# RWKV stage: r and k products dealt out by a table of rounds, and TensorE's order pinned to the program's

## The chip, the cores and the metric

The kernel runs on one core of a Trainium2 chip. The metric is the device time of one execution in microseconds (us); the time of a kernel is the median of several executions. The core has five engines, each with a queue of its own that it works through from the front: TensorE (PE in the profile, with its weight loads as PEld), VectorE (DVE), ScalarE (ACT), GpSimd (POOL) and SyncE (SP), which issues most of the DMAs. Engines wait for each other on semaphores.

## The reference

A decoder trunk of two layers on 256 tokens of width 2048, in float32: one RWKV-7 time-mixing layer and one attention layer, each followed by a squared-ReLU MLP. The change lies in the time mixing, which is

```
xs = h + (token_shift(h) - h) * mu            # six mixtures
r, k, v = xs[0] @ W_r, xs[1] @ W_k, xs[2] @ W_v
decay = exp(-exp(w_log)); a = sigmoid(...); g = sigmoid(xg @ g1) @ g2
for each token t, per head of 64 channels (32 heads):
    sa = S @ (-kk_t)
    S  = S * w_t + sa (kk_t * a_t)^T + v_t k_t^T
    y_t = S @ r_t
out = ((groupnorm(y) + bonus) * g) @ w_o
```

The kernel does not go token by token. It takes the sequence in two chunks of 128 tokens and solves a triangular system in each: products of decayed r, k and kk make 128x128 matrices, a lower triangle is inverted (16x16 blocks first, then 32, 64 and 128 by doubling), and the state S passes from the first chunk to the second.

## The kernel before

The 2048 channels are 16 tiles of 128 (two heads each). A tile's work is the generator `rwkv_tile(i)`, in 27 steps that end at its `yield`s. Three tiles are in flight (`LONG`), each begun nine rounds of the main loop after the one before (`STAGGER`), so that the three stand nine steps apart; nine rounds of the loop are called a round below, and a round in that sense begins one new tile. The steps that matter here, with their products on TensorE by the names of the profile:

- steps 1 to 5: `wa` (decay and a), the scan `cum`, `st`, and the operands AR, bt, kt on VectorE
- step 6: `pm` from bt (L658), made into MB by ScalarE and POOL; step 7: `tr` of bt and kt; step 8: A32, Dg and the four Z on ScalarE and VectorE
- step 9: the two `ar` products from Z (L710), and `pm` from kt
- steps 10 to 12: the X chain, 15 turns of `xt` = ar * X (L722) and X += xt (L723) on VectorE, each of which needs the one before; `pg` (the gate) and the first `prhs` (L739) in between; at its end T16 on ScalarE and Tn on VectorE (L748)
- step 13: `pW` from Tn (L753); steps 14 to 19: `pN`, `pW`, `pT` in turn, the doubling, each through ScalarE or VectorE to the next, to the finished inverse Tt
- steps 20 to 24: `pu`, `psS`, `prhs`, `py`, the solve and the state, chunk by chunk
- steps 25 to 27: the group norm (`tr` of V, mean, var, `yt`) and the output

Since three tiles advance together, a turn of the main loop runs for instance steps 4, 13 and 22.

Beside the tiles go the r and k products of the next tile, `project_rk(i)`: `rk` in the profile. Each of the two has 16 k-tiles of 128 rows, a k-tile is three matmuls (high and low halves of the weights and of the inputs, L213 to L215), so 32 k-tiles and 96 products a tile. The weights are loaded as `raw`, 1024 columns at a time are rounded on ScalarE (`whi`, L162), and the rest is taken off on VectorE (`wlo`, L163), into two buffers (`WB`) that all weights of the stage share. At each such unit `pump` gives VectorE some of the modulation's matrix-vector products, the ada work (L310, `raw` with `crow`, 1024 columns each).

The loop gives `fill`, the generator of the products, a fixed number of turns after each turn of the tiles: 16 / 9, of two k-tiles each.

The program is traced in this order and then handed to a scheduler, which sets each engine's order by its own costs. Only inside `with tc.manual_schedule(engines={PE})` does TensorE's order follow the program's; before, the RWKV stage has no such block. After tile 15 is begun, `fill` is `out_start`, part of the output projection, at `PACE` turns a step.

Of the kernel before, what the change touches and what calls it, by code (L numbers as in the profile page):

```python
# [33 lines left out]
STAGGER = 9  # L34
XV = 2
RATE_R = 0.85
RATE_T = 0.75
PACE = 2.5
RATE_M = 0.68
RATE_L = 0.25  # L40
RATE_H = 1.0
# [35 lines left out]
def trunk_kernel(ctx: ExitStack, tc: tile.TileContext, a, out, dbg=None):  # L77
# [83 lines left out]
    def hilo(hi, lo, x):  # L161
        ACT.copy(hi, x)  # L162
        return DVE.tensor_sub(lo, x, hi.bitcast(F32))  # L163
# [3 lines left out]
    def load(src, n=2048, ahead=False):  # L167
        raw = room_for[0]() if room_for[0] else None
        if raw is not None:
            SP.dma_start(raw[:, :n], src)  # L170
            return raw
        more = split.get("more")
        if more and not ahead:
            split["turn"] += 1
        raw = (more if more and not ahead and split["turn"] > EARLY else wp).tile([P, 2048], F32, tag="raw", name="raw")
        SP.dma_start(raw[:, :n], src)
        return raw
# [5 lines left out]
    def pump(n):  # L183

        due[0] += n
        while due[0] >= 1:
            due[0] -= 1
            if next(ada_it[0], 0) == 0:
                return
# [22 lines left out]
    def mm3w(ps, wh, wl, xh, xl, start, stop):  # L212
        PE.matmul(ps, wh, xh, start=start, stop=False)  # L213
        PE.matmul(ps, wh, xl, start=False, stop=False)  # L214
        PE.matmul(ps, wl, xh, start=False, stop=stop)  # L215
# [162 lines left out]
    with ExitStack() as s0:  # L378
# [8 lines left out]
        def xs_at(w, z, kt):  # L387
            return XS[kt // 4][:, 2 * w + z, kt % 4, :]
# [152 lines left out]
        with ExitStack() as s2:  # L541
# [9 lines left out]
            def tmp(tag, shape=(T,), bufs=1, dt=F32):  # L551
                return p5.tile([P, *shape], dt, tag=tag, name=tag, bufs=bufs)
# [13 lines left out]
            def project_rk(i):  # L566

                ps = banks["rk"].tile([P, 512], F32, tag="rk", name="rk")
                res = []
                for w, name in enumerate(("wr", "wk")):  # L570
                    raw = load(a[name][i])
                    o = slice(w * T, (w + 1) * T)
                    for half in range(2):
                        hi = split["hi"].tile([P, 1024], F32R, tag="whi", name="whi")
                        lo = split["lo"].tile([P, 1024], F32R, tag="wlo", name="wlo")
                        hilo(hi, lo, raw[:, half * 1024 : half * 1024 + 1024])
                        pump(rate[0])
                        for j in range(8):
                            kt = half * 8 + j
                            s = slice(j * P, (j + 1) * P)  # L580
                            mm3w(ps[:, o], hi[:, s], lo[:, s], xs_at(w, 0, kt), xs_at(w, 1, kt), kt == 0, kt == KT - 1)
                            if j % 2:
                                yield
                    res.append(tmp("rk"[w] + "S"))
                    ACT.copy(res[w], ps[:, o])  # L585
                rks[i] = res
# [292 lines left out]
            def out_start():  # L879

                for i in range(KO):
                    split_o(i)
                    yield
                for n in range(4):
                    pss = [banks[k].tile([P, 512], F32, tag=k, name="pos") for k in ("rk", "mm")]
                    for g in range(KO // 4):
                        for half, (hi, lo) in enumerate(unit(a["wo"][n, g])):
                            for j in range(2):
                                kt = g * 4 + half * 2 + j
                                s = slice(j * 512, (j + 1) * 512)  # L890
                                for t in range(2):
                                    q = slice(t * P, (t + 1) * P)
                                    mm3(pss[t], o_h[:, kt, q], o_l[:, kt, q], hi[:, s], lo[:, s], kt == 0, kt == KO - 1)
                                    yield
                    for t in range(2):
                        ACT.copy(yo[:, t, n * 512 : (n + 1) * 512], pss[t])
# [4 lines left out]
            for _ in project_rk(0):  # L901
                pass
            flying, nxt, steps = [], 0, 0
            fill, owed, pace = iter(()), 0.0, 16 / STAGGER
            while nxt < KT or flying:
                if nxt < KT and len(flying) < LONG and steps >= STAGGER * nxt:
                    for _ in fill:
                        pass
                    flying.append(rwkv_tile(nxt))
                    nxt += 1  # L910
                    if nxt < KT:
                        fill = project_rk(nxt)
                    else:
                        o_h = p1.tile([P, KT, T], F32R, tag="xs0", name="oh")
                        o_l = p1.tile([P, KT, T], F32R, tag="xs1", name="ol")
                        yo = p1.tile([P, KT, T], F32R, tag="xs2", name="yo").bitcast(F32).rearrange(
                            "p (t k) c -> p t (k c)", t=2)
                        fill, pace = out_start(), PACE
                        rate[0] = RATE_T
                steps += 1  # L920
                for g_ in list(flying):
                    if next(g_, 0) == 0:
                        flying.remove(g_)

                owed += pace if flying else 48
                while owed >= 1:
                    owed -= 1
                    next(fill, 0)
            for _ in fill:
                pass  # L930
            for i in range(KO, KT):
# [299 lines left out]
    cs = cp.tile([P, 2, 2, 32], F32, name="cs")  # L1231
    rx = mlp(0, x, rx, RATE_M, rotary_tables)
    if dbg:
# [330 lines left out]
```

## Time and profile before

| what | us |
|---|---|
| median of three runs | 2627.69 (2624.5 to 2628.51) |
| the profiled execution | 2610.6 |
| its span | 2608.9 |
| TensorE busy | 2510.7 (96% of the span) |
| VectorE busy | 1950.6 (75%) |
| ScalarE busy | 1314.7 (50%) |
| r and k products (`rk`), first and last start | 212.0 and 683.1 |
| first and last `ar` product of the stage | 244.9 and 714.6 |

A profile line of the timeline reads: start, duration, engine, line, instruction, what is written and read, shape, how often, and in brackets how long the engine stood idle before it and for whom. Matmuls are pipelined and their ends are modelled, so that a run of 256-column products shows 0.28 us for each while one starts every 0.12; the distance of starts is what one costs. In a table of stretches each engine has its busy time and its count of instructions; after the engines come the granted share of TensorE's clock, the busy share of the DMA engines and GB/s.

### The profile page before, as it was taken

How to read it: one execution, taken by the hardware profiler on the slowest of the kernel's cores; microseconds unless marked ns; L12 is line 12 of the kernel's file. 1: busy time of each engine (PE TensorE's matmuls, PEld its weight loads, DVE VectorE, ACT ScalarE, POOL GpSimd, SP SyncE). 2: the span in 40 equal slices, each digit the busy share in tenths (PEclk: the TensorE clock that was granted, in tenths of full speed). 3: DMA queues.
4: the chain of work that ended last, by engine and by line, in shares of the span. 5: the costliest groups of instructions: out<-in, count | busy, mean ns of one | idle time of the engine just before them, and what ended most of it. 6: DMA issues, size and time to landing. Idle time of an engine off the chain costs nothing.

```text
span 2608.9 us, 39245 instructions
## 1 busy us (share of the span) xinstructions
PE 2510.7 (96%) x15048; PEld 2077.0 (80%) x15048; DVE 1950.6 (75%) x3823; ACT 1314.7 (50%) x2361; POOL 65.9 (3%) x150
## 2 busy tenths in 40 slices
PE   6998999999997999999999999999899999999998
PEld 3667888888776888888888878788788888888886
DVE  4797888888877788888888868777677655565555
ACT  4555666666745444444444446544544444444443
POOL 0000111011100000000000000000000000000000
PEclk9999999999999999999999999999999999999999
DMA  9755444444466588888888834657657555555553
GB/s 374 304 192 202 155 170 157 166 158 171 167 227 258 201 337 316 329 332 325 333 316 331 328 140 139 211 178 263 219 210 260 192 193 187 187 191 194 187 186 127
DMA packets 87885, 594.54 MB, mean 228 GB/s; under 512 B 10128, under 2 KB 14480, under 8 KB 16784
## 3 DMA queue, kind: packets, MB, share of 16 engines
q1 hardware_dynamic: 87696, 592.03, 62.9%
q8 instruction: 118, 1.93, 0.3%
q14 instruction: 71, 0.58, 0.1%
HBM read 589.89 MB, written 2.10 MB: 227 GB/s over the span
## 4 chain that ended last, share of the span: by engine, by line
PE 87%; DVE 7%; ACT 3%; DMA 2%; issue 1%; POOL 0%; SPq 0%; DVEq 0%; ACTq 0%
PE pup L223 17%; PE pd L208 9%; PE pd L210 9%; PE pd L209 9%; PE pup L224 9%; PE rk L213 2%; PE rk L215 2%; PE rk L214 2%; PE pm L658 2%; DVE wlo L163 2%; PE po L209 1%; PE po L210 1%; PE po L208 1%; PE pv L209 1%; PE pv L210 1%
## 5 line engine op out<-in xcount | busy, mean ns | idle before, releaser
L162 ACT CAST whi<-raw 128x1024 fp32r<-128x1024 f32 x729 | 743.7, 1023 | 882.7 <-PE pd L210 356.3
L163 DVE TENSOR_TENSOR wlo<-raw,whi 128x1024 fp32r<-128x1024 f32 x729 | 865.2, 1189 | 430.1 <-ACT whi L162 427.0
L223 PE MATMUL pup<-h,whi 128*128 128x512 f32 x1920 | 677.8, 398 | 0.0
L224 PE MATMUL pup<-h,wlo 128*128 128x256 f32 x1920 | 539.7, 281 | 0.0
L223 PEld LDWEIGHTS pup<-h,whi 128*128 128x128 f32 x1920 | 361.0, 188 | 88.2
L208 PE MATMUL pd<-whi,uh 128*128 128x512 f32 x1024 | 399.2, 390 | 0.0
L210 PE MATMUL pd<-whi,ul 128*128 128x512 f32 x1024 | 398.9, 390 | 0.0
L209 PE MATMUL pd<-wlo,uh 128*128 128x512 f32 x1024 | 398.8, 389 | 0.0
L310 DVE SCALAR_TENSOR_TENSOR raw<-raw,crow 128x1024 f32<-128x1024 f32 x320 | 388.5, 1221 | 10.5 <-DMA raw<-in_adat_dram 10.2
L224 PEld LDWEIGHTS pup<-h,wlo 128*128 128x128 f32 x1920 | 363.4, 189 | 0.5
L210 PEld LDWEIGHTS pd<-whi,ul 128*128 128x128 f32 x1024 | 192.3, 188 | 40.2
L208 PEld LDWEIGHTS pd<-whi,uh 128*128 128x128 f32 x1024 | 192.3, 188 | 39.9
L209 PEld LDWEIGHTS pd<-wlo,uh 128*128 128x128 f32 x1024 | 192.3, 188 | 39.5
L213 PE MATMUL rk<-xs,whi 128*128 128x256 f32 x512 | 155.2, 303 | 2.8 <-ACT rS L585 2.2
L215 PE MATMUL rk<-xs,wlo 128*128 128x256 f32 x512 | 149.6, 292 | 2.0 <-DVE wlo L163 2.0
L214 PE MATMUL rk<-xs,whi 128*128 128x256 f32 x512 | 147.1, 287 | 0.0
L213 PEld LDWEIGHTS rk<-xs,whi 128*128 128x128 f32 x512 | 98.5, 192 | 13.8 <-issue 8.9
L215 PEld LDWEIGHTS rk<-xs,wlo 128*128 128x128 f32 x512 | 98.4, 192 | 4.7 <-DVE wlo L163 2.8
L214 PEld LDWEIGHTS rk<-xs,whi 128*128 128x128 f32 x512 | 98.5, 192 | 0.9
L722 DVE TENSOR_TENSOR xt<-ar,X 128x60 f32<-128x60 f32 (+14 forms) x240 | 49.5, 206 | 17.5 <-ACT ar L711 14.8
L1180 DVE TENSOR_TENSOR ya<-pd,ya 128x512 f32<-128x512 f32 x96 | 61.5, 682 | 0.0
L209 PE MATMUL pv<-wlo,xsv 128*128 128x512 f32 x128 | 52.8, 413 | 5.5 <-DVE wlo L163 5.3
(431 smaller groups left out, 3671.3 us busy)
## 6 DMA issues: line engine op xcount, KB each, us to landing
raw<-in_adat_dram SPq DMA_DIRECT2D x160, 1024.0 KB, 6.9
raw<-in_up_dram SPq DMA_DIRECT2D x128, 1024.0 KB, 4.9
raw<-in_dn_dram SPq DMA_DIRECT2D x128, 1024.0 KB, 4.9
early<-in_ada_dram SPq DMA_DIRECT2D x17, 1024.0 KB, 11.6
raw<-in_wr_dram SPq DMA_DIRECT2D x16, 1024.0 KB, 4.9
raw<-in_wk_dram SPq DMA_DIRECT2D x16, 1024.0 KB, 5.0
raw<-in_wo_dram SPq DMA_DIRECT2D x16, 1024.0 KB, 5.8
raw<-in_mo_dram SPq DMA_DIRECT2D x16, 1024.0 KB, 4.9
```

The lines of the kernel that those rows point to most:

```text
L162: ACT.copy(hi, x)
L163: return DVE.tensor_sub(lo, x, hi.bitcast(F32))
L208: PE.matmul(ps, lh, rh, start=start, stop=False)
L209: PE.matmul(ps, lh, rl, start=False, stop=False)
L210: PE.matmul(ps, ll, rh, start=False, stop=stop)
L213: PE.matmul(ps, wh, xh, start=start, stop=False)
L214: PE.matmul(ps, wh, xl, start=False, stop=False)
L215: PE.matmul(ps, wl, xh, start=False, stop=stop)
L223: PE.matmul(ps, hi[:, s], x2[:, kt].rearrange("p e t -> p (e t)"), start=(kt == 0), stop=False)
L224: PE.matmul(ps[:, T:], lo[:, s], x2[:, kt, 0, :], start=False, stop=(kt == KT - 1))
L310: DVE.scalar_tensor_tensor(raw[:, s], raw[:, s], 1.0, crow[:, s], ALU.mult, ALU.mult, accum_out=part[:, kt, half : half + 1])
L1180: DVE.tensor_add(y, pss[t], y)
```

## The change

Three edits, all in the main loop of the RWKV stage and in `project_rk`. `project_rk` yields after every k-tile instead of every second. While `fill` is `project_rk` (that is up to the turn in which tile 15 is begun, `pace` 0), the number of k-tiles after a turn of the tiles comes from the table `LEAN` by the turn's place in its round, 32 in all, instead of a steady share. And in the same turns the steps of the tiles and the products are traced inside a manual schedule for TensorE, one block for each turn.

```
+LEAN = (6, 3, 3, 3, 5, 2, 4, 6, 0)
...
                             mm3w(ps[:, o], hi[:, s], lo[:, s], xs_at(w, 0, kt), xs_at(w, 1, kt), kt == 0, kt == KT - 1)
-                            if j % 2:
-                                yield
+                            yield
...
-            fill, owed, pace = iter(()), 0.0, 16 / STAGGER
+            fill, owed, pace = iter(()), 0.0, 0
             while nxt < KT or flying:
                 if nxt < KT and len(flying) < LONG and steps >= STAGGER * nxt:
-                    for _ in fill:
-                        pass
+                    with nullcontext() if pace else tc.manual_schedule(engines={mybir.EngineType.PE}):
+                        for _ in fill:
+                            pass
                     flying.append(rwkv_tile(nxt))
...
+                with nullcontext() if pace else tc.manual_schedule(engines={mybir.EngineType.PE}):
+                    for g_ in list(flying):
+                        if next(g_, 0) == 0:
+                            flying.remove(g_)
+
+                    owed += (pace or LEAN[steps % STAGGER]) if flying else 48
+                    while owed >= 1:
+                        owed -= 1
+                        next(fill, 0)
                 steps += 1
-                for g_ in list(flying):
-                    if next(g_, 0) == 0:
-                        flying.remove(g_)
-
-                owed += pace if flying else 48
-                while owed >= 1:
-                    owed -= 1
-                    next(fill, 0)
```

The engines have the same instructions before and after, and outside the stage in the same order. In the changed program lines from L583 on are one higher, those of the helpers two. TensorE's order around a tile's `pW` from Tn, here of tile 12 (names: `rk` the r and k products, `T_7832` that tile's T16). Before:

```order
L215 MATMUL rk<-xs,wlo 128x256
L753 MATMUL pW<-Tn,A_7620 32x16 x16
L213 MATMUL rk<-xs,whi 128x256
L214 MATMUL rk<-xs,whi 128x256
L215 MATMUL rk<-xs,wlo 128x256
L658 MATMUL pm<-AR,kt 128x256
L762 MATMUL pN<-T_7832,W 32x32 x16
L872 MATMUL yt<-ident,tha 128x128 x2
L873 MATMUL yt<-rb,kc 128x256
L658 MATMUL pm<-AR,kt 128x256
L777 MATMUL pW<-T_7935,MB 32x32 x4
```

Ahead of this `pW` stand 87 of the round's 96 `rk` products, counted from the tile's `ar`, and 9 between it and the next tile's `ar`. Now, in the same place:

```order
L217 MATMUL rk<-xs,wlo 128x256
L816 MATMUL prhs<-S,AR 128x128
L819 MATMUL prhs<-V,MK 128x64 x2
L839 MATMUL py<-S,AR 128x128
L754 MATMUL pW<-Tn,A_8006 32x16 x16
L633 MATMUL st<-kc,bt 128x2 x2
L215 MATMUL rk<-xs,whi 128x256
L216 MATMUL rk<-xs,whi 128x256
L217 MATMUL rk<-xs,wlo 128x256
```

`pW` now stands in its turn of the loop, between step 22 of the oldest tile (`prhs`, `py`) and step 4 of the youngest (`st`), with 36 `rk` products between the `ar` and it and 60 behind it; that holds for every pinned round.

VectorE's order at the end of the same tile's X chain. Before:

```order
L851 TENSOR_SCALAR mean<-mean 128x4
L310 SCALAR_TENSOR_TENSOR raw,adpart<-raw,crow 128x1024
L722 TENSOR_TENSOR xt<-ar,X 128x4x2
L860 TENSOR_TENSOR tha<-py,mean 128x256
L723 TENSOR_TENSOR X<-X,xt 128x4x2
L722 TENSOR_TENSOR xt<-ar,X 128x4
L163 TENSOR_TENSOR wlo<-raw,whi 128x256
L723 TENSOR_TENSOR X<-X,xt 128x4
L864 TENSOR_REDUCE var<-th 128x4
L865 TENSOR_SCALAR var<-var 128x4
L141 TENSOR_SCALAR rsy<-var 128x4
L748 STREAM_TRANSPOSE Tn<-T_7832 128x128
```

And now:

```order
L165 TENSOR_TENSOR wlo<-raw,whi 128x1024
L724 TENSOR_TENSOR X<-X,xt 128x4x5
L312 SCALAR_TENSOR_TENSOR raw,adpart<-raw,crow 128x1024
L723 TENSOR_TENSOR xt<-ar,X 128x4x4
L724 TENSOR_TENSOR X<-X,xt 128x4x4
L723 TENSOR_TENSOR xt<-ar,X 128x4x3
L724 TENSOR_TENSOR X<-X,xt 128x4x3
L723 TENSOR_TENSOR xt<-ar,X 128x4x2
L724 TENSOR_TENSOR X<-X,xt 128x4x2
L723 TENSOR_TENSOR xt<-ar,X 128x4
L724 TENSOR_TENSOR X<-X,xt 128x4
L749 STREAM_TRANSPOSE Tn<-T_8241 128x128
```

The group norm of the oldest tile (mean, tha, var) and a `wlo`, which stood between the last turns of the X chain, are behind Tn now, and the last eight X instructions follow each other. From the first `xt` to Tn the stretch held 59 instructions for this tile and holds 47.

## The prediction

> **What bounds the kernel now.** I read the page first, then the same engines in stretches of time, then TensorE and VectorE instruction by instruction over one round of the RWKV stage.
>
> ```profile
> span 2608.9 us, 39245 instructions
> PE 2510.7 (96%) x15048; PEld 2077.0 (80%) x15048; DVE 1950.6 (75%) x3823; ACT 1314.7 (50%) x2361; POOL 65.9 (3%) x150
> ```
>
> TensorE (PE) is nearly always busy, so whatever makes PE wait in the changed stage lengthens the run. Outside that stage the two programs issue the same instructions in the same order; all that follows is about the stage, and there about one round (nine steps of the loop, one new tile). The stretches below are thirteen rounds together, and one of them cut in two at the first product that needs a finished X (tile 12: from its `ar` products to `pW` L753, and from there to the next tile's `ar`).
>
> ```profile
> core 0: us, PE busy (x) PEld busy (x) DVE busy (x) ACT busy (x) POOL busy (x), PEclk, DMA share, GB/s
> 273.10:681.40 408.30, 397.35 (x3907) 337.80 (x3906) 341.37 (x1143) 270.30 (x737) 49.14 (x92) 1.00 0.48 164
> 620.71:643.35 22.64, 21.76 (x173) 19.43 (x172) 20.07 (x66) 15.11 (x39) 1.85 (x4) 1.00 0.40 134
> 643.35:652.13 8.78, 8.78 (x129) 6.37 (x130) 7.56 (x24) 5.52 (x17) 1.87 (x3) 1.00 0.48 178
> ```
>
> A round takes 408.30 / 13 = 31.41 us, and PE (397 us) and VectorE (DVE, 341 us) both fill it. POOL, ScalarE and the DMA engines (share 0.48) have room. The same two stretches for the r and k products alone:
>
> ```profile
> 620.71:643.35 22.64, 11.87 (x87) 10.76 (x87) 0.38 (x1) 1.00 0.40 134
> 643.35:652.13 8.78, 1.86 (x9) 1.25 (x9) 0.00 (x0) 1.00 0.48 178
> ```
>
> 87 of the 96 products of a round stand ahead of `pW`, 9 behind it. Now PE and DVE at the ends of those stretches:
>
> ```profile
> 620.71 1.56 PE L710 MATMUL ar<-Z,kc 128*128 128x384 f32 x4
> ...
> 643.35 0.88 PE L753 MATMUL pW<-Tn,A 32*32 32x16 f32 x32
> ...
> 652.13 0.91 PE L710 MATMUL ar<-Z,kc 128*128 128x384 f32 x2
> ```
>
> ```profile
> 622.82 0.22 DVE L722 TENSOR_TENSOR xt<-ar,X 128x60 f32<-128x60 f32 x1 [1.45 <-ACT ar L711]
> 623.08 0.22 DVE L723 TENSOR_TENSOR X<-X,xt 128x60 f32<-128x60 f32 x1
> 623.33 0.22 DVE L722 TENSOR_TENSOR xt<-ar,X 128x56 f32<-128x56 f32 x1
> ...
> 637.77 1.22 DVE L163 TENSOR_TENSOR wlo<-raw,whi 128x1024 fp32r<-128x1024 f32 x1
> 638.90 0.16 DVE L723 TENSOR_TENSOR X<-X,xt 128x12 f32<-128x12 f32 x1
> ...
> 642.99 0.31 DVE L748 STREAM_TRANSPOSE Tn<-T 128x128 f32<-128x128 f32 x1
> ```
>
> `pW` needs Tn, Tn needs the last of 30 dependent X instructions, and those begin 2.11 us after `ar` (622.82 - 620.71). DVE's queue threads other work between them, so the X chain lasts 20.17 us (622.82 to 642.99), and `pW` follows 0.36 us later. Nothing waits for this chain today: PE has 22.6 us of other work to do in the meantime, and both arrive together. That balance is what the change touches.
>
> **The change, part by part.** Nothing is added or removed: the engines get the same instructions, and every DMA too. Three things move.
>
> *The products.* In the new order 36 r and k products stand between a tile's `ar` and its `pW` in every pinned round, and 60 behind. Before, 58 to 87 stood ahead (tiles 1 to 13, mean 73). With them `st`, one pair of `pu`, four `py`, and two pairs of `tr` go from ahead of `pW` to behind it. One r or k product costs the distance from one start to the next:
>
> ```profile
> 628.45 0.28 PE L213 MATMUL rk<-xs,whi 128*128 128x256 f32 x1
> 628.57 0.28 PE L214 MATMUL rk<-xs,whi 128*128 128x256 f32 x1
> ...
> 632.67 0.56 PE L632 MATMUL st<-kc,bt 128*128 128x2 f32 x4
> 633.09 0.36 PE L213 MATMUL rk<-xs,whi 128*128 128x256 f32 x1
> ...
> 634.60 0.55 PE L825 MATMUL pu<-rh,Tt 128*128 128x64 f32 x4
> 634.99 0.44 PE L838 MATMUL py<-S,AR 128*128 128x128 f32 x2
> ...
> 635.94 0.43 PE L843 MATMUL py<-U,MB 128*128 128x64 f32 x2 [0.30 <-ACT U L827]
> ...
> 636.86 0.36 PE L213 MATMUL rk<-xs,whi 128*128 128x256 f32 x1
> 637.06 0.28 PE L214 MATMUL rk<-xs,whi 128*128 128x256 f32 x1
> ```
>
> So 0.12 us each (628.45 to 628.57); `st` 0.42, `pu` 0.39, `py` 0.92 (each to the next start), and the two `tr` pairs about 0.4 together, estimated from the 0.12 us of a product of twice the columns and one of the slower f32. For tile 12 that is 51 x 0.12 + 2.1 = 8.2 us moved. PE's work ahead of `pW` falls from 22.6 to 14.4 us, and the work behind it grows from 8.78 to 17.0. I take off 0.4 us there, since the products now stand in fewer and longer runs, and the first step of a run takes 0.20 instead of 0.12 (636.86 to 637.06). **Behind `pW`: 16.6 us**, with ends 15.4 (every such joint gone) and 18.0 (below).
>
> *The X chain.* DVE's order follows PE's, and for tile 12 twelve instructions leave the stretch from the first xt to Tn: one `wlo` of 1024 columns (637.77 to 638.90: 1.13 us), six of 256 columns and five of 4. Four raw halves of the ada work (1.2 us each) and three `wlo` stay.
>
> ```profile
> 629.77 1.22 DVE L310 SCALAR_TENSOR_TENSOR raw<-raw,crow 128x1024 f32<-128x1024 f32 x1
> ...
> 633.87 0.17 DVE L635 RECIPROCAL rinv<-rinv 128x4 f32<-128x4 f32 x1
> 633.96 0.40 DVE L638 TENSOR_TENSOR AR<-rS,cum 128x256 f32<-128x256 f32 x1
> ...
> 634.36 0.42 DVE L644 TENSOR_TENSOR bt<-th,tha 128x256 f32<-128x256 f32 x1
> 634.70 0.17 DVE L723 TENSOR_TENSOR X<-X,xt 128x24 f32<-128x24 f32 x1
> ```
>
> By these, 1.13 + 6 x 0.34 + 5 x 0.1 = 3.7 us go. The last eight X instructions then follow each other directly, which costs 0.25 us a step (623.08 to 623.33) where an instruction of another chain hid part of it: about 0.6 back. So `ar` to `pW` needs 2.11 + 20.17 - 3.7 + 0.6 + 0.36 = 19.5 us. Nine of the thirteen rounds have four raw halves in the stretch, two have two and two have one: 0.8 fewer on the mean, 0.9 us. Against that, `wlo` can start only after the cast into one of two buffers, which the products of the half before must have left, and PE reaches those later: 0 to 1.6 us, I take 0.4. **`ar` to `pW`: 19.0 us**, ends 17.8 and 20.5.
>
> *The pin.* PE would have its 14.4 us done some 4.6 us before Tn exists. It can't take the 60 products first: behind the waiting `pW` in its queue stand `st`, nine products, `pu`, `pN` and so on. DVE waits for `st` (rinv, then bt), ScalarE for `pu`, and the cast of the k weights for buffers that those products hold.
>
> The round becomes 19.0 + 16.6 = 35.6 us against 31.41: 4.2 more, in 13 rounds 55 us. Tile 0, with one tile beside it, moves 45 products (81 to 36) but has little PE work: +2 (ends 0 and 4). From step 135 on nothing is pinned; 0.
>
> *The clock.* A wait of 4.6 us in each round is new here, and PE's clock does not like it:
>
> ```profile
> 1563.58 1.22 PE L1022 MATMUL trt<-dg,xr 128*128 128x128 f32 x4 [4.95 <-DVE dg L1319]
> ...
> 24.15 1.08 PE L287 MATMUL adap<-early,c 128*32 128x512 f32 x4 [2.91 <-DVE rsy L158]
> ```
>
> ```profile
> 1562.87:1569.70 6.83, 6.12 (x28) 6.12 (x29) 6.39 (x19) 4.70 (x10) 0.13 (x2) 0.50 0.03 10
> ```
>
> ```profile
> 23.46:30.29 6.83, 5.10 (x24) 0.63 (x24) 4.39 (x14) 1.23 (x3) 0.10 (x1) 0.50 1.01 416
> ```
>
> After a gap of 4.95 us, and after one of 2.91, the granted clock (the column ahead of the DMA share) was 0.50 for 6.83 us, some 6 us of it after the gap. A product then takes 0.21 us instead of 0.12, as the stage itself shows where its clock dipped:
>
> ```profile
> 297.06 0.42 PE L215 MATMUL rk<-xs,wlo 128*128 128x256 f32 x1
> 297.28 0.41 PE L213 MATMUL rk<-xs,whi 128*128 128x256 f32 x1
> ```
>
> That would lose up to 6 x (1 - 0.12 / 0.21) = 2.6 us a round, and 0 if the clock holds. I take 1.6, since some rounds wait less than 3.5 us and the small products behind `pW` are bound by more than the clock: 21 us. The Trainium skill ("TensorE: Matmul & The Clock Gate", section "What's actually happening") has the clock halve after an idle window of about 3.4 us that runs freely; a wait of 4.6 us holds a whole one about a third of the time, which by that rule makes the term 7 us and the sum 14 lower. The gap of 2.91 us above is shorter than that window and was followed by the half clock all the same, so I go by the rows.
>
> **The sum.** 55 + 2 + 21 = 78 us. The profiled execution took 2610.6 us (its span and 1.7 around it), 17 less than the median of the runs shown, 2627.69; it would become 2689, and the median **2706 us**.
>
> **The rivals.** *The clock holds*: the wait as worked out, without the 21 us: 2685. For it: only gaps of nearly 3 us and more show the drop so clearly, and rounds with few raw halves wait less. *A second wait*: behind `pW` the next `ar` needs Z, made from the `pm` products through ScalarE, POOL and DVE:
>
> ```profile
> 637.74 1.14 PE L658 MATMUL pm<-AR,bt 64*128 64x256 f32 x8
> ...
> 647.74 0.28 DVE L704 TENSOR_TENSOR Z<-Dg,kc 128x128 f32<-128x128 f32 x1
> ```
>
> From the end of `pm` (638.88) to the last Z (648.02) are 9.1 us; in the new order 36 products (4.3 us) and some 3 us of small ones stand between. If the chain can't be quicker than today, PE waits 1.7 us more, 22 us in 13 rounds: 2728; that is the 18.0 above. *Faster*: fewer changes between kinds of products and no wait. It decides at one place: if the X chain, `ar` to `pW`, takes no more than PE's 14.4 us, PE stays full. Then the 11 us in which PE idles (408.30 - 397.35) and about 5 us of joints could go: 2612. Against it: DVE would have to drop another 4.6 us from a stretch whose instructions stand in its queue in that order. *No change*: the pin holds inside a step only, so the scheduler might have kept today's balance; the order shows that it did not.
>
> **How the numbers follow.** The wait with the clock drop 0.57 (2706), with the clock held 0.24 (2685), with the second wait 0.10 (2728), faster 0.06 (2612), no change 0.03. Within 0.2%, 5 us, is about what a measurement of this kernel can't tell from no change. Faster 0.06, same 0.03, slower 0.91. The range takes the first three with their ends: 17.8 + 15.6 without a clock drop (2.0 x 13 + 2 = 28) gives 2656, 19.0 + 18.0 with 2.3 of clock (7.9 x 13) gives 2730. 2656 to 2735.
>
> **What would show it.** Right: PE waits for Tn ahead of the `pW` group for some 3 to 6 us in most rounds of the new trace, a granted clock under 1.00 in the stage, rounds of 35 to 38 us, and nothing different after the stage. Wrong: PE busy through the stage with `pW` waiting for nothing; an X chain much shorter than 16 us; or rounds of 31 us and less.

## The result, and the profile after

The changed kernel took 2761.81 us (median of four runs, 2761.23 to 2772.8) against 2626.9 in the runs beside it: a ratio of 1.0526, 95% interval 1.049 to 1.0563. It is slower by 135 us; 79 were forecast (2706), and the time lies above the range of 2656 to 2735. The sign and the place were right, the size was not.

The page of the changed kernel, with TensorE's granted clock over the 40 slices (before, every slice read 9):

```profile
span 2759.7 us, 39216 instructions
PE 2581.3 (94%) x15048; PEld 2147.5 (78%) x15048; DVE 1974.3 (72%) x3823; ACT 1317.0 (48%) x2361; POOL 64.9 (2%) x150
PEclk8998878789879999999999999999999999999999
```

Each digit is a slice of 69 us in tenths. The clock falls in the slices of the RWKV stage (the fourth to the twelfth; the first reads 8 too, ahead of the change), and what comes after the stage is as before. The same work, thirteen rounds from tile 1's `ar` to tile 14's, as a stretch of time, and one of those rounds cut in two at `pW`:

```profile
293.60:831.50 537.90, 455.07 (x3903) 399.67 (x3901) 364.84 (x1143) 272.89 (x741) 49.02 (x91) 0.84 0.35 123
705.30:723.50 18.20, 13.42 (x102) 11.19 (x100) 15.83 (x51) 11.21 (x27) 1.53 (x4) 0.99 0.52 190
723.50:745.90 22.40, 21.87 (x201) 19.67 (x201) 11.10 (x36) 9.53 (x29) 1.43 (x3) 0.70 0.24 75
```

A round takes 41.37 us (537.90 / 13, to the rounding of the ends); it took 31.41. The thirteen lost 129.6 us (537.90 - 408.30). 71.9 of them are TensorE standing (537.90 - 455.07 = 82.8 against 10.95), and 57.7 are the same products taking longer (455.07 against 397.35) at a clock of 0.84; the ends of products are modelled, so that this split is an estimate. Cut at `pW` over all thirteen rounds, `ar` to `pW` takes 19.73 us and `pW` to the next `ar` 21.64.

The waits of TensorE in those rounds (microseconds in total, how often, the longest):

```profile
PE pW L754 <- DVE Tn L749: 42.2, 13, 4.1
PE rk L217 <- DVE wlo L165: 13.0, 12, 1.6
PE pu L826 <- ACT Tt L807: 10.5, 13, 0.8
PE pN L786 <- ACT Tt L788: 6.9, 13, 0.9
PE psS L835 <- ACT S L837: 4.3, 4, 1.1
PE rk L215 <- ACT whi L164: 3.9, 13, 0.3
PE rk L215 <- ACT rS L586: 1.9, 2, 1.0
```

The longest in the same view of before:

```profile
PE pu L825 <- ACT Tt L806: 6.2, 13, 0.6
```

The wait for Tn is half of the 82.8 us. The other half is a list of small ones, 10.5 us of it at `pu`, where 6.2 us stood before too: six further hand-overs between TensorE and other engines stand in it. One dip of the clock, in TensorE's timeline behind one `pW`:

```profile
720.69 0.44 PE L839 MATMUL py<-S,AR 128*128 128x128 f32 x2
723.54 1.32 PE L754 MATMUL pW<-Tn,A 32*32 32x16 f32 x32 [2.41 <-DVE Tn L749]
...
726.03 0.41 PE L216 MATMUL rk<-xs,whi 128*128 128x256 f32 x1
726.24 0.41 PE L217 MATMUL rk<-xs,wlo 128*128 128x256 f32 x1
...
738.13 0.28 PE L216 MATMUL rk<-xs,whi 128*128 128x256 f32 x1
738.25 0.28 PE L217 MATMUL rk<-xs,wlo 128*128 128x256 f32 x1
```

A product starts every 0.21 us (726.03 to 726.24) until about 737, some 13 us after the wait, and every 0.12 us (738.13 to 738.25) from there.

### The profile page after: what moved, and what is told of

Same layout as the page of the kernel before. It is cut to its first block, busy times and chain, and to the rows that moved or that the text cites. A ratio compares the mean times of both kernels' runs of the same rounds, so it can differ in the third digit from the quotient of the medians.

```text
span 2759.7 us, 39216 instructions
## 1 busy us (share of the span) xinstructions
PE 2581.3 (94%) x15048; PEld 2147.5 (78%) x15048; DVE 1974.3 (72%) x3823; ACT 1317.0 (48%) x2361; POOL 64.9 (2%) x150
## 4 chain that ended last, share of the span: by engine, by line
PE 62%; DVE 3%; ACT 1%; issue 0%; DVEq 0%; ACTq 0%
PE pup L225 16%; PE pd L210 8%; PE pd L212 8%; PE pd L211 8%; PE pup L226 8%; PE po L211 1%; PE po L212 1%; PE po L210 1%; PE pl L210 1%; PE pl L212 1%; PE pl L211 1%; PE psc L1423 1%; PE pkq L215 1%; PE psc L1422 1%; PE pup L212 1%; PE pkq L216 1%
## 5 line engine op out<-in xcount | busy, mean ns | idle before, releaser
L215 PE MATMUL rk<-xs,whi 128*128 128x256 f32 x512 | 176.3, 344 | 10.1 <-ACT rS L586 5.1
L217 PE MATMUL rk<-xs,wlo 128*128 128x256 f32 x512 | 164.5, 321 | 15.8 <-DVE wlo L165 15.8
L216 PE MATMUL rk<-xs,whi 128*128 128x256 f32 x512 | 162.3, 317 | 0.0
L215 PEld LDWEIGHTS rk<-xs,whi 128*128 128x128 f32 x512 | 115.6, 226 | 23.2 <-ACT whi L164 7.2
L217 PEld LDWEIGHTS rk<-xs,wlo 128*128 128x128 f32 x512 | 116.5, 227 | 18.2 <-DVE wlo L165 18.2
L216 PEld LDWEIGHTS rk<-xs,whi 128*128 128x128 f32 x512 | 117.0, 229 | 0.0
L754 PE MATMUL pW<-Tn,A 32*32 32x16 f32 x512 | 18.4, 200 | 48.9 <-DVE Tn L749 48.8
```

## The experiments

All run as the changed kernel does but for the edit shown, against runs of the kernel before on the same chip. "Round", "standing" and "clock" are those of the same thirteen rounds in the profiled execution.

| kernel | us | ratio, 95% interval | round, us | PE standing, us | clock |
|---|---|---|---|---|---|
| before | 2626.9 | 1 | 31.41 | 11.0 | 1.00 |
| after | 2761.81 | 1.0526, 1.049 to 1.0563 | 41.37 | 82.8 | 0.84 |
| table alone | 2635.73 | 1.0039, 1.0019 to 1.0059 | 32.47 | 13.1 | 0.94 |
| pin alone | 2756.64 | 1.0494, 1.0465 to 1.0522 | 40.64 | 66.9 | 0.83 |
| 24 useless products | 2744.18 | 1.0446, 1.0423 to 1.0469 | 40.22 | 52.5 | 0.89 |
| table early, pinned | 2734.69 | 1.0409, 1.0384 to 1.0433 | 39.01 | 70.6 | 0.88 |
| tiles pinned, products free | 2722.9 | 1.0369, 1.0344 to 1.0393 | 38.62 | 53.3 | 0.85 |
| no ada in the rounds | 2810.48 | 1.07, 1.0666 to 1.0734 | 37.94 | 64.0 | 0.90 |
| 36 useless products | 2733.79 | 1.0401, 1.0369 to 1.0432 | 39.31 | 51.0 | 0.96 |
| early table, no pin | 2681.46 | 1.0209, 1.0184 to 1.0235 | 35.06 | 31.6 | 0.92 |
| each tile pinned by itself | 2639.36 | 1.0064, 1.0043 to 1.0084 | 32.38 | 23.2 | 0.98 |
| tiles pinned, newest first | 2706.93 | 1.0305, 1.027 to 1.034 | 36.84 | 39.8 | 0.89 |

**The table without the pin.**

```
-                with nullcontext() if pace else tc.manual_schedule(engines={mybir.EngineType.PE}):
+                with nullcontext():
```

(and the same where the rest of `fill` is taken)

> The changed kernel with the table but without the pin: the scheduler orders TensorE again, and 62 to 91 of the 96 products stand ahead of pW from Tn, as before the change. Theory (the pin puts pW ahead of too little work, the wait for Tn halves the clock): rounds near 31.4 us, no wait at pW, 2627 within 10 us. Rival (the table itself, that is when the weights are loaded, cast and subtracted, is at fault): most of the 135 us stays, over 2690.

Measured: 2635.73 us. The rounds as one stretch:

```profile
282.10:704.30 422.20, 409.06 (x3905) 346.73 (x3903) 338.47 (x1144) 270.65 (x741) 47.07 (x93) 0.94 0.45 157
```

A round is 1.06 us longer than before, and TensorE stands hardly more (13.1 us). The rest of the difference is the clock of 0.94, at which TensorE is busy for 409.06 us instead of 397.35. The table makes about a tenth of the rounds' loss, or less: the execution of the kernel before that was profiled (2610.6 us) was 17 us faster than the median of its runs, and by the medians the table costs 9.3 us.

**The pin without the table.**

```
-                    owed += (pace or LEAN[steps % STAGGER]) if flying else 48
+                    owed += (pace or 32 / STAGGER) if flying else 48
```

> The pin without the table: 32/9 k-tiles after every turn, 42 products ahead of pW and 54 behind. Theory: six products fewer behind than with the table (0.7 us at full clock) and as much more cover, so the wait is some 3 us instead of 3.7 and mostly long enough to halve the clock: 2725 to 2765. Rival (the table is at fault): back near 2630 to 2660.

Measured: 2756.64 us, all but 5 us of the whole change. With an even share 42 products stand ahead of `pW` and 54 behind, and the first wait is the same:

```profile
PE pW L754 <- DVE Tn L749: 37.6, 13, 5.4
```

So the loss comes with the pin, whatever the table.

**24 useless products ahead of `pW`**, whose results nothing reads, to fill the wait for Tn.

```
+WARM = 24
...
+                for _ in range(WARM if i < 14 else 0):
+                    PE.matmul(pW[:, T:], sg_h[:, 0, :P], sg_h[:, 1, :], start=True, stop=True)
```

> The changed kernel with 24 useless products (128x128 by 256 columns, 0.12 us each, 2.9 us in all) ahead of pW in the 14 pinned tiles, written to unused columns of pW's own bank; the result is unchanged. VectorE's order is the same as in the changed kernel, and so is Tn's time. Theory (the half clock behind the wait costs 5 us a round): PE stays active through the wait, the granted clock stays at or near 1.00 in the stage, the stretch behind pW falls from 21.9 to about 17 us, and the kernel gets faster by up to 13 x 5 = 65 us: 2690 to 2720 in spite of 40 us of added work. Rival (the stretch behind pW is long because of further waits in the pinned order, and the clock is only a sign of them): within 10 us of the changed kernel, 2755 to 2775, or slower.

Measured: 2744.18 us; more work, and 18 us faster than the changed kernel. That lies between the theory's 2690 to 2720 and the rival's 2755 to 2775, and neither came out whole. The wait for Tn fell from 42.2 to 10.0 us. Four of the thirteen rounds now have no half clock behind `pW`, most of the others some 10 us, and that stretch takes 20.05 us on the mean (some 17 were expected); a stretch from `pW` to the next `ar` of either kind:

```profile
352.00:369.90 17.90, 16.52 (x204) 14.64 (x203) 10.96 (x36) 9.53 (x29) 1.63 (x4) 1.00 0.27 89
389.65:410.75 21.10, 20.61 (x201) 18.69 (x201) 11.36 (x35) 9.51 (x29) 2.38 (x3) 0.76 0.26 88
```

This gives the price of the clock. A mean of 0.76 over 21.10 us is 10.1 us at half; they cost 21.10 - 17.90 = 3.2 us, 0.31 us for each microsecond at half clock. It depends on what runs in that time: in the kernel with 36 useless products the stretches with 3.4 us at half take 19.34 us, 1.45 more than those with none, which is 0.43.

**36 useless products**, the same edit with `WARM = 36`.

> As the kernel with 24 useless products, with 36 (4.3 us, more than the mean wait for Tn was). There, rounds without a halved clock had 17.9 us behind pW, and those with 10.2 us of it 21.1. Theory (the gap ahead of pW starts the halving): with the gap closed most rounds have 17.9, ar to pW grows by 0.5 us at most, and 19 us of further useless work bring the time down again, to 2715 to 2735. Rival (the small products behind pW halve the clock by themselves): no gain, 2740 to 2760.

Measured: 2733.79 us, and the mechanism is as expected: the wait for Tn is gone (one of 0.8 us is left in thirteen rounds), the clock in the rounds is 0.96, and eight of them have no half clock behind `pW`. (`ar` to `pW` is 0.7 us longer than with 24, where 0.5 at most was expected.) One stretch behind `pW`:

```profile
635.05:652.95 17.90, 16.67 (x203) 14.72 (x203) 11.74 (x36) 9.53 (x29) 1.64 (x4) 1.00 0.39 135
```

The kernel's wait for Tn and its three longest waits over the thirteen rounds:

```profile
PE pW L757 <- DVE Tn L750: 0.8, 1, 0.8
PE rk L218 <- DVE wlo L166: 13.2, 13, 1.6
PE rk L216 <- ACT rS L587: 11.6, 13, 1.0
PE pu L829 <- ACT Tt L810: 10.5, 13, 0.8
```

With the clock nearly whole and no wait for Tn, a round still takes 39.31 us, 7.9 more than before. Of the 7.9, 3.1 are TensorE standing (51.0 us in thirteen rounds against 11.0), nearly all at the other hand-overs, and 4.3 are the useless products themselves. So the wait for Tn and the clock drop behind it aren't the whole of the loss.

**The products early in the round, pinned**, so that 72 stand ahead of `pW` and 24 behind, about as before the change.

```
-LEAN = (6, 3, 3, 3, 5, 2, 4, 6, 0)
+LEAN = (10, 8, 6, 2, 2, 0, 2, 2, 0)
```

> The changed kernel with another table, (10, 8, 6, 2, 2, 0, 2, 2, 0): the pin stays, but 72 products stand ahead of pW and 24 behind, the mean of the order before the change. Theory (the number of products ahead of pW decides): cover 14.4 + 4.3 = 18.7 us against an X chain of 19 to 20.4 (one more wlo in it), a wait of at most 1.5 us, no halved clock, 12.3 us behind pW: rounds of 31.5 to 33, 2630 to 2655. Rival (a pinned order waits elsewhere whatever the table): over 2690.

Measured: 2734.69 us. The 2630 to 2655 us of the theory were missed, and its rival (a pinned order waits elsewhere) came true: the wait for Tn went (3.0 us are left), and others came in its place (the first five rows):

```profile
PE pN L786 <- ACT Tt L788: 19.4, 13, 1.7
PE pu L826 <- ACT Tt L807: 10.5, 13, 0.8
PE psS L835 <- ACT gS L734: 9.3, 13, 0.7
PE rk L215 <- ACT rS L586: 8.7, 9, 1.1
PE rk L217 <- DVE wlo L165: 6.6, 9, 1.2
```

TensorE stands 70.6 us in all. How many products stand ahead of `pW` decides where it waits, and only a little of how long.

**The tiles pinned, the products free.**

```
-                    owed += (pace or LEAN[steps % STAGGER]) if flying else 48
-                    while owed >= 1:
-                        owed -= 1
-                        next(fill, 0)
+                owed += (pace or LEAN[steps % STAGGER]) if flying else 48
+                while owed >= 1:
+                    owed -= 1
+                    next(fill, 0)
```

(The rest of `fill` is taken unpinned as well. Both edits to the products are also in the last two kernels of this section, where they are not shown again.)

> The changed kernel with the table; the steps of the tiles stay pinned turn by turn, but the r and k products are traced outside the block, so that the scheduler may put them into gaps. 44 to 91 of them (mean 66) stand ahead of pW, more where the scheduler saw Tn late. Theory (what costs is that PE can't take products while it waits): most of the loss is gone, rounds of 32 to 34 us, 2635 to 2670. Rival (the pinned order of the tiles' own steps is at fault, by waits on ScalarE at pN, pu and psS): rounds over 36 us, over 2690.

Measured: 2722.9 us. The 2635 to 2670 us of the theory were missed, and its rival (the pinned order of the tiles' own steps costs most) came true. TensorE stands at other places than those that the rival named, `pu` apart. The wait for Tn is not in the list any more; these are (the first five rows):

```profile
PE rk L215 <- ACT rS L586: 13.4, 12, 1.5
PE rk L217 <- DVE wlo L165: 9.8, 10, 1.6
PE pu L826 <- ACT Tt L807: 9.6, 13, 0.8
PE ar L711 <- DVE Z L705: 8.2, 8, 2.5
PE yt L873 <- DVE tha L869: 6.6, 5, 2.5
```

**No ada work in the rounds.** It leaves VectorE's queue in the rounds, which shortens the X chain, and is done after the stage.

```
-            rate[0] = RATE_R
+            rate[0] = 0.0
```

> The changed kernel, pin and table, with no ada work on VectorE in the pinned rounds (it is done later in the kernel, so the whole time is not the measure, the rounds are). Three raw halves of 1.14 us leave the X chain's stretch on the mean. Theory (the wait at pW is that stretch): ar to pW falls from 19.7 to about 16.2 us, the wait at pW from 3.2 to under 1 us, fewer halved clocks, rounds of 34 to 37 us instead of 41.4. Rival (other waits of the pinned order take over): ar to pW stays over 18, rounds over 39.

Measured: 2810.48 us. The whole is slower because the moved work lengthens what follows the stage (from tile 14's `ar` to the end 2031.5 us, in the changed kernel 1928.2). In the rounds the theory was right in direction and too bold in size: `ar` to `pW` takes 17.77 us instead of 19.73 (16.2 was expected), a round 37.94 (34 to 37). The first two waits:

```profile
PE rk L217 <- DVE wlo L165: 21.4, 13, 1.7
PE pW L754 <- DVE Tn L749: 13.5, 13, 1.0
```

So the ada work in VectorE's queue is part of what sets the end of the X chain and the wait for Tn; with that shorter, the wait for `wlo` is the longest.

**The early table without the pin.**

```
-LEAN = (6, 3, 3, 3, 5, 2, 4, 6, 0)
+LEAN = (10, 8, 6, 2, 2, 0, 2, 2, 0)
...
-                with nullcontext() if pace else tc.manual_schedule(engines={mybir.EngineType.PE}):
+                with nullcontext():
```

> The table (10, 8, 6, 2, 2, 0, 2, 2, 0) without the pin, in search of a version that beats both: the scheduler puts 72 to 85 products ahead of pW. Theory (PE's own work and the X chain must end together): cover 19 to 20 us, 10 to 12 behind, rounds of 31 to 32 us, 2615 to 2640, a gain of 0.4% at most. Rival (an early table takes products from the gaps of the last steps): rounds over 32.5, 2640 to 2660.

Measured: 2681.46 us, where 2615 to 2640 was expected: a miss, and above the rival's 2660 too. TensorE stands 31.6 us in the rounds, in many small waits, at a clock of 0.92. An uneven table costs something without the pin too, this one 2%, that of the change 0.4%. Why the early one costs five times as much stays open.

**Each tile's step pinned by itself.** TensorE keeps the order inside each tile's step; the steps of different tiles, and the products, may pass each other.

```
-                with nullcontext() if pace else tc.manual_schedule(engines={mybir.EngineType.PE}):
-                    for g_ in list(flying):
+                for g_ in list(flying):
+                    with nullcontext() if pace else tc.manual_schedule(engines={mybir.EngineType.PE}):
                         if next(g_, 0) == 0:
                             flying.remove(g_)
```

> The pin is laid around each tile's step singly (its own instructions keep their order), and neither the order of the tiles against each other nor the products are pinned; the table stays. In the order 49 to 77 products stand ahead of pW. With the three tiles' steps pinned one behind the other the kernel took 2723 us, with the table and no pin 2636. Theory: the order of one tile's step against the others' is at fault, since TensorE then stands at the hand-overs of one tile (Tt, rS, wlo, Z) while another tile's ready product is queued behind. Here they may pass each other again: 2625 to 2665 us, rounds of 31.5 to 33.5 us, granted clock 0.97 or more, each of those waits under 7 us in 13 rounds. Rival: the order inside a step is at fault already (a step's own product and the one that needs its result): 2690 to 2730 us, with pu waiting for Tt some 10 us and rk for rS some 13 as with the tiles pinned.

Measured: 2639.36 us, as the theory had it, and the rival fell. The thirteen rounds as a stretch:

```profile
280.00:700.90 420.90, 397.66 (x3902) 339.02 (x3901) 345.70 (x1141) 268.32 (x738) 43.62 (x91) 0.98 0.44 154
```

And the first two waits in it:

```profile
PE pu L826 <- ACT Tt L807: 10.5, 13, 0.8
PE rk L217 <- DVE wlo L165: 4.3, 7, 1.0
```

The wait for rS (13.4 us with the tiles pinned) is not in the list any more, that of `ar` for Z falls from 8.2 us to 0.6. Only `pu` waits as long as when the tiles are pinned, 0.8 us a round, where under 7 us in all was expected. It waited 6.2 us before the change, 7.7 with the table alone and 5.9 with the pin alone; what makes it 10.5 here isn't shown.

**The tiles pinned, the newest first**, products free.

```
-                    for g_ in list(flying):
+                    for g_ in list(flying)[::-1]:
```

> The tiles' steps are pinned one behind the other, the products free, as in the kernel that took 2723 us, but the newest tile's step stands first in each turn and the oldest last. Theory: any written order of whole steps keeps TensorE waiting at several hand-overs in each round, whichever tile comes first, and the clock falls after them: 2685 to 2780 us, TensorE idle for 40 us or more over the 13 rounds, granted clock 0.96 or less. Rival: only the order with the oldest tile first is at fault, because the newest tile's long X chain starts last: 2625 to 2665 us, TensorE idle for some 15 us.

Measured: 2706.93 us, standing 39.8 us (479.00 - 439.25), clock 0.89 in the rounds: inside the theory's range of time, just under its 40 us of standing, and far from the rival's 2665. The stretch:

```profile
282.50:761.50 479.00, 439.25 (x3891) 372.34 (x3890) 341.56 (x1129) 271.62 (x737) 43.90 (x91) 0.89 0.40 137
```

And its first wait:

```profile
PE rk L215 <- ACT rS L586: 9.7, 11, 1.4
```

The other order of the tiles costs some 15 us less and waits in part at other places, but it waits. Both orders cost over 80 us against the kernel before, so one tile in a bad place doesn't explain the loss.

**What the runs make of the cause.** Between neighbours that differ in one thing, a round grows from 31.41 us to 32.47 with the table, stays at 32.38 when each tile's own step is pinned, rises to 38.62 when the three tiles' steps are pinned one behind the other, and to 41.37 when the products are pinned among them too: +1.1, -0.1, +6.2, +2.8. By the medians against the runs beside each, the same four steps are +9, +6, +82 and +37 us; with profiled executions up to 17 us from their medians, the two small ones can't be told from nothing by the rounds. Nearly two thirds of the loss is the order of the tiles against each other, and a pinned block as such costs little. Each step holds what the scheduler made of the other engines' orders too: some 800 of VectorE's 3823 instructions stand elsewhere when the tiles are pinned one behind the other, but about as many (750) do when each tile's own step is pinned, which costs 6 us. No kernel here beat the one before.

## Why the prediction was right and wrong

The wait that the prediction named came, and the chain behind it took as long as worked out. What failed are two terms of the sum that were too small, the clock and the work behind `pW`, and a stretch ahead of tile 1 that was hardly priced; so rounds of 35 to 38 us, one of its signs, became 41.4.

**Right: the place and the chain.** TensorE waits for Tn ahead of `pW` in every round, 42.2 / 13 = 3.2 us (4.6 was forecast; 3 to 6 in most rounds was the sign given, and nine of the thirteen waits are 3.9 to 4.1 us, the others 1.0 to 2.4). The wait is shorter because TensorE already stood some 2.1 us a round earlier in the same stretch, at `wlo`, `pu` and `whi` (13.0 + 10.5 + 3.9 over 13); the X chain sets the end either way. `ar` to `pW` was forecast at 19.0 us. It took 19.73 with 2.3 us of half clock in it (the clock's record cut at `ar` and `pW`, as for the 11.1 us below); less 2.3 x 0.31 that is 19.0, an estimate that single rounds bear out: with at most 0.4 us of half clock there, a round with four raw halves in the chain takes 19.74 us, one with two 18.21, one with a single half 17.15, and weighted as in the prediction (nine, two and two rounds) that is 19.1. The X chain of the round shown, which has two:

```profile
707.44 0.22 DVE L723 TENSOR_TENSOR xt<-ar,X 128x60 f32<-128x60 f32 x1 [0.92 <-ACT ar L712]
...
723.17 0.31 DVE L749 STREAM_TRANSPOSE Tn<-T 128x128 f32<-128x128 f32 x1 [0.65 <-ACT T L745]
```

Right too: the stretch after the stage differs by 0.7 us, and the balance moved as the order showed.

**Wrong: the clock term**, 1.6 us a round (21 us). By the row of the thirteen rounds, 537.90 x (1 - 0.84) x 2 = 172 us ran at half clock, 13 us a round; at 0.31 that is 4.1 us a round, 53 in all. The price of a microsecond came out lower than the prediction's 0.43 (1 - 0.12 / 0.21); its duration was the error. I took 6 us from two gaps far from this stage, where the half clock ended some 6 us after the gap; here it went on for 10 to 15 us behind `pW` in eleven of the thirteen rounds, and for 3.4 in the two whose wait for Tn was 1.0 us. Ahead of `pW` come 2.3 us a round that the term didn't have at all.

**Wrong: the work behind `pW`**, 16.6 us. In the round at full clock above (17.90) TensorE is busy for 16.52 us, so the count of products and joints was right. What it left out is 1.4 us of standing, 0.9 at `rk` for rS and 0.5 at `pN` for Tt. That round is of the kernel with 24 useless products; in the changed kernel itself `pN` waits as much, while the wait for rS shows in two rounds only (1.9 us): at half clock TensorE comes to it later, so that a part of the standing is hidden in the slow clock. Over the thirteen rounds, 21.64 less 11.1 x 0.31 is 18.2: 1.6 us a round more than forecast, 21 in all. Against the 17.9 us of the rounds at full clock it would be 1.3 a round and 17, and the clock 4.4 a round; the split between the two terms is an estimate, their sum is measured. The prediction looked for a second wait at one place, the `ar` for Z, and found it unlikely; that wait didn't come, and several others did. Its sentence on the pin named what is queued behind the waiting `pW` but priced only that one wait, while other hand-overs had lost their cover too.

**Wrong: what lies ahead of tile 1**, +2 us. It was +20.5. Tile 0 from `ar` to `ar`, before and after, and the turns ahead of it from the first `rk`:

```profile
244.90:273.10 28.20, 24.54 (x259) 20.94 (x257) 24.14 (x72) 17.98 (x47) 3.84 (x6) 1.00 0.56 196
212.00:244.90 32.90, 27.46 (x201) 25.18 (x200) 22.53 (x44) 16.95 (x35) 1.38 (x3) 0.95 0.59 217
```

```profile
254.12:293.60 39.48, 28.85 (x249) 24.59 (x247) 23.58 (x72) 18.12 (x48) 2.75 (x6) 0.78 0.39 135
215.40:254.10 38.70, 32.75 (x213) 29.45 (x212) 22.99 (x45) 17.14 (x35) 1.38 (x3) 0.87 0.54 195
```

Tile 0 grew by 11.3 us, of which TensorE's standing is 7.0 (10.6 against 3.7) and the rest its slower clock; the turns before its first `ar`, which are pinned as well and which the sum left out, by 5.8. The first `rk` itself came 3.4 us later, in a part that the change doesn't touch; in the other runs it came at 214.0 to 219.4 us.

**The sum.** The prediction's 2689 for a profiled execution became 2761.4 (the span and 1.7). The misses: clock 33 (4.15 - 1.6 a round), behind `pW` 21, ahead of tile 1 18.5, in all 72. The correction of 17 us from the profile to the median was not needed: the profiled execution after stands at its median, so 17 of those 72 don't show in the distance from 2706. Two slips in the range are small beside that: its low end takes 15.6 us behind `pW` where the prediction gives 15.4, and its high end leaves out the X chain's own upper end of 20.5, which alone is 1.5 us a round, 20 in all.

The rivals: the faster and the unchanged kernel fell as argued; "the clock holds" fell in every round (3.4 us at half clock behind `pW` at the least). Its argument, that only gaps of nearly 3 us and more show the drop clearly, doesn't fit the dip at 297 us, whose products the prediction itself shows: no gap stands ahead of it (last section). The second wait came as several, none of them at Z.

## What to carry to other kernels

An order of TensorE written out over several independent chains took from many hand-overs here the other chains' work that hid them: price all hand-overs on the pinned path, not the largest alone, and pin each chain by itself if the order inside it is what matters. Moving the filler about moved the waits; those that went at one place came back in part at others. Where a stage's own traces show the clock drop after short waits, as here after 1 to 4 us, add the products behind each at the slow clock, by the time that the clock stays low in that stage.

## What the hardware did that was not expected

The half clock doesn't need a long gap, or any, and it lasts. In the kernel before, the one dip of the thirteen rounds came behind a stretch in which TensorE was busy all the time by the profile, with many small products (the stretch ahead of the drop, and the one behind it):

```profile
293.12:296.53 3.41, 3.41 (x73) 2.68 (x71) 2.87 (x7) 1.79 (x5) 0.74 (x2) 1.00 0.36 72
296.53:299.94 3.41, 3.41 (x22) 3.12 (x22) 1.41 (x7) 2.23 (x9) 0.64 (x1) 0.50 0.70 279
```

In the kernel with 36 useless products TensorE stood for 0.96 us at an `rk`, and the clock halved just behind it (the same two stretches):

```profile
478.79:482.20 3.41, 2.45 (x25) 2.10 (x24) 3.41 (x7) 3.13 (x8) 0.00 (x0) 1.00 0.02 5
482.21:485.61 3.40, 3.40 (x23) 2.94 (x23) 1.39 (x4) 0.67 (x2) 0.00 (x0) 0.50 0.65 178
```

The wait, in the timeline:

```profile
481.51 0.39 PE L216 MATMUL rk<-xs,whi 128*128 128x256 f32 x1 [0.96 <-ACT rS L587]
```

In the changed kernel, behind the `pW` shown above, it stayed at half for 13.64 us in which TensorE was busy for 13.25:

```profile
723.15:736.79 13.64, 13.25 (x122) 12.40 (x122) 7.55 (x23) 4.37 (x12) 0.15 (x1) 0.50 0.19 56
```

The Trainium skill ("TensorE: Matmul & The Clock Gate", section "What's actually happening") puts the half clock after an idle window of about 3.4 us and the full one after one busy window of that length. These rows agree with neither: 2.45 us of work in 3.41, and 3.41 in 3.41, did not keep the full clock, and 13.25 in 13.64 did not soon bring it back.

The clock's record of each of the twelve traces changes only at multiples of 3.41 us from its first change. In the changed kernel, counted over these steps from 200 us to 860, in 38 of the 39 steps at half clock that another followed, products of fewer than 3072 columns together were started (a 128x256 has 256), and in all 20 that the full clock followed of 3072 or more, while TensorE was busy for 3.41 us in the median step of both kinds. Over all twelve traces it is less clean: 217 of 238 and 146 of 185. So the columns that the products stream go with the return of the clock better than the busy time does; many 32x32 and 64-column products give few of them. No run here changes that alone, and what sets the length isn't shown.
